# The output projection as seven block products over pairs of token tiles, with its sums and low parts spread over VectorE, ScalarE and GpSimd

## The chip, the core and the metric

The kernel runs on one NeuronCore of one Trainium2 chip. TensorE does the matrix products, VectorE (DVE in the profile), ScalarE (ACT) and GpSimd (POOL) do elementwise work, SyncE (SP) issues the DMAs. The metric is the time of one execution on the device, in microseconds (us). The kernel before takes 676.48 us in the median of three runs (676.13 to 676.74).

## The reference

One encoder layer on 1024 tokens of 1024 channels, in float32. After a LayerNorm `h`, one input projection gives the inputs of two branches, 2-D neighbourhood attention and a bidirectional RG-LRU. The part that the change touches is the end:

```python
y_a = attn * jax.nn.silu(z_a)
y_b = h * jax.nn.silu(z_b)
m = jax.nn.sigmoid(g_a + b_merge[0]) * (y_a @ w_ba) + jax.nn.sigmoid(g_b + b_merge[1]) * (y_b @ w_bb)
out = m @ w_out
return layer_norm(ALPHA * x + out, ln_g, ln_b)
```

`m` and `w_out` are 1024 x 1024, and the sum over channels is the last large product of the kernel.

## The kernel before

Every large product is made in three passes of a reduced-precision float32 format. A matrix is split into a high part (a cast, on ScalarE) and a low part (the full value minus the high part, `lo_of`, line 128). `mm3` (line 130) then issues three matmuls for each 128-channel piece: high x high, low x high and high x low, all added up in one PSUM bank of 128 x 512.

The input projection, up to about 425 us, is already done with seven block products in place of eight. Attention follows, with the products of the second branch filled in between, up to 535 us.

Then comes the **merge**, 16 slots (loop at line 1316). Slot 2j+n makes channels 128j to 128j+127 of `m` for token half n: 12 matmuls into a bank `mb`, then on VectorE the gate (`b_gate`, line 1020) and the sum with the other branch (`merge`, line 1302), on ScalarE the high part `mh`, on VectorE the low part `ml`. Between these ScalarE and GpSimd split the next slot's branch weights (`wb`) and the rows of `w_out` (`wo`, 128 x 1024 at a time, ScalarE line 1344, GpSimd line 128).

Then comes the **output projection** (loop at line 1390): for each of the 8 tiles of 128 tokens two column halves, each of 8 channel pieces x 3 = 24 matmuls (`o_product`, line 1365). The last tile's second half is done in two pieces of 256 columns. VectorE adds ALPHA times the residual (`z`, line 1399) and takes the statistics. For tiles 0 to 6, ScalarE scales (line 1408), GpSimd multiplies by the gain and adds the bias (lines 1409 and 1410) and SyncE stores the tile (line 1411). The last tile is finished on VectorE alone (lines 1416 and 1421), in four pieces that are stored one by one (line 1422).

The order of the instructions of VectorE, ScalarE, GpSimd and SyncE is that of the code (`tc.manual_schedule`): each engine works its list in order, and an instruction whose input is not there holds up all behind it. TensorE's list is in the order of the code too.

Of the kernel before, what the change touches and what calls it, by code (L numbers as in the profile page):

```python
# [10 lines left out]
F32 = mybir.dt.float32  # L11
# [56 lines left out]
def encoder_kernel(ctx, tc, x, gb1, gb, w_qk, w_v, w_s, w_ba, w_bb, w_gate, smalls, bias, w_out, out):  # L68
# [1009 lines left out]
    ya = pair(yap, [P, 4, S], "ya")  # L1078
    at0 = pool("at0")
    acc = [pst.tile([P, HALF], F32, name=f"acc{g}") for g in range(2)]  # L1080
# [104 lines left out]
    def gated(h, n):  # L1185
        hp = h // 2
        at_, (hi, lo) = attns[hp][:, halves[n]], [t[:, hp, halves[n]] for t in ya]
        G.tensor_tensor(at_, at_, gates[hp][:, halves[n]], ALU.mult)
        G.tensor_copy(hi, at_)
        lo_of(G, lo, at_, hi)  # L1190

    def last_half(g):
# [3 lines left out]
        def product(n):  # L1196
            at_ = attns[hp][:, halves[n]]
            V.tensor_tensor(at_, at_, gates[hp][:, halves[n]], ALU.mult)
            A.copy(ya[0][:, hp, halves[n]], at_)

        def low(n):
            lo_of(V, ya[1][:, hp, halves[n]], attns[hp][:, halves[n]], ya[0][:, hp, halves[n]])
# [23 lines left out]
    for unit in range(-NT, H * NT + PV_LAG):  # L1226
# [50 lines left out]
        if unit == H * NT:  # L1277
# [4 lines left out]
            wo = [pair(wop, [P, D], f"wo{k}") for k in range(NK - 2)]  # L1282
            wos = {}

            def w_load(k):
                if k < NK:
                    wos[k] = wop.tile([P, D], F32, tag="wos", bufs=3, name=f"wos{k}")
                    SP.dma_start(wos[k][:], w_out[k * P:(k + 1) * P, :])
# [4 lines left out]
            for k in range(3):  # L1293
                w_load(k)
# [3 lines left out]
    sums_m, mh, ml = {}, {}, {}  # L1298

    def merge(j, n, o):  # L1300
        b_gate(0, j, n, o)
        V.tensor_tensor(o[:], o[:], late["m", j, n][:], ALU.add)
        mh[j, n] = late["mp"].tile([P, HALF], F32R, tag=f"m{j}{n}", name=f"mh{j}{n}")
        A.copy(mh[j, n][:], o[:])

    def merge_lo(j, n, o):
        lo_of(V, ml[j, n][:], o[:], mh[j, n][:])
# [6 lines left out]
    banks[0] = pst  # L1314
    turns.append(itertools.chain(["mb", "mb", "s"], itertools.cycle(["tp", "mb", "s"])))
    for slot in range(2 * NK + 2):
        j, n = divmod(slot, 2)
        if 2 < slot <= 2 * NK:
            merge(*divmod(slot - 1, 2), sums_m[slot - 1])
        if slot == 2:  # L1320
            at0.release()
            mlp = pool("mlp")
            ml.update({(j, n): mlp.tile([P, HALF], F32R, name=f"ml{j}{n}") for j in range(NK) for n in range(2)})
            wo += [pair(mlp, [P, D], f"wo{k}") for k in range(NK - 2, NK)]
            merge_lo(0, 0, sums_m.pop(0))
        for q in (1,) if slot == 3 else (slot - 2,) if slot > 3 else ():
            merge_lo(*divmod(q, 2), sums_m.pop(q))
        if j < NK:
            if n == 0:
                b_load(0, j + 2)  # L1330
            g_load(0, j + 1, n, **(dict(tag=f"u{slot % 4}", bufs=1) if slot % 4 else dict(tag="z", bufs=5)))
            o = sums_m[slot] = bank(f"mb{j}{n}")

            run(b_group(0, j, n, ya, o, range(3 if slot < 2 else 4)))
            if 0 < slot < 3:
                run(b_group(0, 0, slot - 1, ya, sums_m[slot - 1], range(3, 4)))
            if n == 0 and j > 0:
                b_split(0, j + 1, A)
            if 0 < slot < 3:
                merge(0, slot - 1, sums_m[slot - 1])  # L1340

        if slot % 2:
            if j < NK:
                A.copy(wo[j][0][:], wos[j][:])
# [4 lines left out]
        if slot == 9:  # L1349
            zp = pool("zp")  # L1350
            gb2 = zp.tile([P, 2, D], F32, name="gb2")
            zs = {}

            def load_z(i):
                if i < NT:
                    zs[i] = zp.tile([P, D], F32, tag="z", bufs=4, name=f"z{i}")
                    SP.dma_start(zs[i][:], h_d[i])

        elif slot in (10, 12, 14):
            load_z(slot // 2 - 5)  # L1360
        elif slot in (11, 13):
            SP.dma_start(gb2[:, :, halves[slot // 13]], gb[slot // 13])
# [9 lines left out]
    def small(name, n, bufs=2):  # L1372
        return zp.tile([P, n], F32, tag=name[:2], bufs=bufs, name=name)

    def newton(mv, i, other):

        sd, ve = small(f"sd{i}", 1), small(f"ve{i}", 3)
# [12 lines left out]
    for i in range(NT):  # L1390
        last = i == NT - 1
# [117 lines left out]
```

## Time and profile before

| what | us |
| --- | --- |
| median of three runs | 676.48 |
| the profiled execution | 676.07 |
| its span, first to last instruction | 674.3 |
| merge: 192 matmuls, from 535.19 | 43.59 |
| output projection: 408 matmuls, from 578.77 | 87.36 |

In the rows that follow, a group row of the timeline gives the start, the duration, the engine, the line, the operation, out<-in, the shapes and the count; in brackets the idle time before it and what ended it. The chain of waits gives start, duration and the work that the end of the program hung on. The window rows give, for each stretch of the span, its length and then the busy time of each engine with the number of instructions.

### The profile page before, as it was taken

How to read it: one execution, taken by the hardware profiler on the slowest of the kernel's cores; microseconds unless marked ns; L12 is line 12 of the kernel's file. 1: busy time of each engine (PE TensorE's matmuls, PEld its weight loads, DVE VectorE, ACT ScalarE, POOL GpSimd, SP SyncE). 2: the span in 40 equal slices, each digit the busy share in tenths (PEclk: the TensorE clock that was granted, in tenths of full speed). 3: DMA queues.
4: the chain of work that ended last, by engine and by line, in shares of the span. 5: the costliest groups of instructions: out<-in, count | busy, mean ns of one | idle time of the engine just before them, and what ended most of it. 6: DMA issues, size and time to landing. Idle time of an engine off the chain costs nothing.

```text
span 674.3 us, 9352 instructions
## 1 busy us (share of the span) xinstructions
PE 663.7 (98%) x3189; PEld 554.3 (82%) x3189; DVE 498.9 (74%) x835; ACT 364.5 (54%) x615; POOL 354.4 (53%) x261
## 2 busy tenths in 40 slices
PE   8999999999999999999999999999999999999995
PEld 7888888888888887888788888888888888888884
DVE  6978876985998699879968785477788787443334
ACT  6555433357786676669576634477777555210110
POOL 5898263433676575567647544115255456334432
PEclk9999999999999999999999999999999999999999
DMA  8746616033344033531543557998794467412211
GB/s 322 246 152 228 209 41 221 36 125 109 126 143 150 22 108 110 172 126 48 202 172 124 172 186 261 339 332 308 251 317 146 163 232 280 170 62 94 93 63 62
DMA packets 48990, 113.40 MB, mean 168 GB/s; under 512 B 5088, under 2 KB 9776, under 8 KB 47408
## 3 DMA queue, kind: packets, MB, share of 16 engines
q1 hardware_dynamic: 48912, 112.81, 48.0%
q8 instruction: 25, 0.41, 0.2%
q14 instruction: 21, 0.17, 0.1%
q10 hardware_dynamic: 32, 0.01, 0.0%
HBM read 77.11 MB, written 35.68 MB: 167 GB/s over the span
## 4 chain that ended last, share of the span: by engine, by line
PE 76%; DVE 9%; issue 4%; POOL 1%; ACT 1%; DMA 1%; SPq 0%; DVEq 0%; POOLq 0%
PE a L134 28%; PE o L134 13%; PE mb L134 13%; PE s L134 11%; PE acc L1145 4%; PE s L1099 3%; PE pt L1121 3%; PE g L794 2%; POOL ht_l L128 1%; DVE ws_l L128 1%; DVE wa_l L128 1%; DMA a_2f<-in_w_s_dram 1%; DVE uc L752 1%; ACT ht_h L312 1%; DVE s_12f L384 0%
## 5 line engine op out<-in xcount | busy, mean ns | idle before, releaser
L134 PE MATMUL a<-ht_h,ws_h 128*128 128x512 f32 x136 | 53.1, 391 | 0.0
L134 PE MATMUL a<-ht_h,ws_l 128*128 128x512 f32 x136 | 53.0, 389 | 0.0
L134 PE MATMUL a<-b_h,wa_l 128*128 128x512 f32 x136 | 53.0, 389 | 0.0
L134 PE MATMUL a<-ht_l,ws_h 128*128 128x512 f32 x136 | 52.9, 389 | 0.0
L134 PE MATMUL a<-b_h,wa_h 128*128 128x512 f32 x136 | 52.9, 389 | 0.0
L134 PE MATMUL a<-b_l,wa_h 128*128 128x512 f32 x136 | 52.9, 389 | 0.0
L134 PE MATMUL o<-wo_h,ml 128*128 128x512 f32 (+1 forms) x136 | 51.2, 377 | 0.0
L134 PE MATMUL o<-wo_l,mh 128*128 128x512 f32 (+1 forms) x136 | 51.2, 376 | 0.0
L134 PE MATMUL o<-wo_h,mh 128*128 128x512 f32 (+1 forms) x136 | 51.2, 376 | 0.0
L1109 DVE CUSTOM_DVE_ANT_0 sc<-s,bias 128x384 f32<-128x384 f32 (+1 forms) x64 | 33.3, 522 | 21.5 <-PE s L1099 14.1
L1399 DVE SCALAR_TENSOR_TENSOR z<-z,o 128x512 f32<-128x512 f32 (+1 forms) x17 | 11.2, 656 | 51.1 <-PE o L134 51.1
L1129 ACT CAST pt_h<-pt 128x384 fp32r<-128x384 f32 x64 | 29.0, 453 | 25.3 <-PE pt L1121 17.3
L1409 POOL TENSOR_TENSOR z<-z,gb 128x1024 f32<-128x1024 f32 x7 | 16.8, 2397 | 48.6 <-ACT z L1408 48.6
L1114 ACT ACTIVATE p<-sc,summ 128x384 f32<-128x384 f32 (+1 forms) x64 | 37.8, 591 | 5.5 <-DVE summ L1109 5.3
L1378 ACT ACTIVATE sd<-mv,eps_z 128x1 f32<-128x1 f32 x8 | 2.4, 294 | 67.1 <-DVE mv L1404 67.1
L128 DVE TENSOR_TENSOR pt_l<-pt,pt_h 128x384 fp32r<-128x384 f32 x64 | 33.2, 519 | 2.1 <-ACT pt_h L1129 1.6
L326 PE MATMUL v<-wv,b_h 128*128 128x512 f32 x128 | 32.8, 398 | 0.2 <-ACT b_h L279 0.2
L902 POOL CAST wb_h<-wb 128x512 fp32r<-128x512 f32 x9 | 7.0, 778 | 49.3 <-DMA wb<-in_w_bb_dram 49.3
L128 POOL TENSOR_TENSOR ht_l<-t,ht_h 128x512 fp32r<-128x512 f32 x16 | 22.0, 1408 | 19.9 <-ACT ht_h L312 19.9
L1099 PE MATMUL s<-ks,qs 128*128 128x384 f32 (+1 forms) x128 | 31.5, 327 | 0.0
L134 PEld LDWEIGHTS a<-ht_h,ws_h 128*128 128x128 f32 x136 | 25.5, 188 | 5.9 <-issue 0.4
L1121 PEld LDWEIGHTS pt<-ident,p 128*128 128x128 f32 x176 | 23.1, 140 | 8.5
(455 smaller groups left out, 2192.4 us busy)
## 6 DMA issues: line engine op xcount, KB each, us to landing
ks<-k_d SPq DMA_DIRECT2D x8, 1024.0 KB, 8.3
h_d<-x SPq DMA_DIRECT2D x8, 512.0 KB, 5.0
v_d<-vs SPq DMA_DIRECT2D x8, 512.0 KB, 3.5
q_d<-q SPq DMA_DIRECT2D x8, 512.0 KB, 3.0
ga_d<-ga SPq DMA_DIRECT2D x16, 256.0 KB, 2.2
gb_d<-gb SPq DMA_DIRECT2D x16, 256.0 KB, 2.4
k_d<-k SPq DMA_DIRECT2D x8, 512.0 KB, 3.4
qs<-q_d SPq DMA_DIRECT2D x8, 512.0 KB, 5.2
```

Source lines behind the costliest of these rows:

```text
L128: eng.tensor_tensor(lo, full, hi.bitcast(F32), ALU.subtract)
L134: PE.matmul(o, a, b, start=first and i == 0, stop=last and i == len(prods) - 1, skip_group_check=not (first and last))
L326: PE.matmul(vos[i][:], a, wv[kind == "w"][k][:], start=vn[i] == 0, stop=vn[i] == 23)
L794: PE.matmul(o[:, n, :], w[:, 2 * d + b, :], us[b][:, n * HALF:(n + 1) * HALF], start=z == 0, stop=z == 1)
L1099: PE.matmul(o[:, :P * len(near(t))], q[:, t * P:(t + 1) * P], k[:, z, keys], start=z == 0, stop=z == 1)
L1109: V.tensor_tensor_reduce(s[:, :w], o[:, :w], heads[h][2][:, b0:b0 + w], -1.0, 3.0e38, ALU.add, ALU.min, accum_out=sums[h][0][:, t:t + 1])
L1114: A.activation(probs[h % 2][t][:], scs.pop((h, t))[:, :w], AF.Exp, bias=sums[h][0][:, t:t + 1], scale=-1.0, accum_out=sums[h][1][:, t:t + 1])
L1121: PE.transpose(tp[:, n * P:(n + 1) * P], probs[h % 2][t][:, z * P:(z + 1) * P], ident[:])
L1129: A.copy(pt[0][:, span(b)], tps[h, b][:, :P * len(near(b))])
L1145: PE.matmul(acc[g][:, d:d + w], vvs[h // 2][:, b, h % 2, :], pt[:, a:a + w], start=b in (1, 6) and z == 0, stop=z == 1 and b == (4, 7)[g])
L1399: V.scalar_tensor_tensor(z[:, cols], z[:, cols], ALPHA * TWICE, o, ALU.mult, ALU.add)
L1409: G.tensor_tensor(z[:], z[:], gb2[:, 0, :], ALU.mult)
```

## The change

The 1024 x 1024 product is cut into 2 x 2 blocks of 512. With A the merged `m` (rows are token halves 1 and 2, columns are channel halves) and B = `w_out`:

- S1 = A21 + A22, S2 = S1 - A11, S3 = A11 - A21, S4 = A12 - S2
- T1 = B12 - B11, T2 = B22 - T1, T3 = B22 - B12, T4 = B21 - T2
- C11 = A11 B11 + A12 B21; with U2 = A11 B11 + S2 T2 and U3 = U2 + S3 T3: C12 = U2 + S1 T1 + S4 B22, C21 = U3 + A22 T4, C22 = U3 + S1 T1

That is seven products where the four blocks of C need eight. Each is done for the four pairs p (token tiles p and p + 4), 28 in all, each of 4 channel pieces x 3 = 12 matmuls into one bank. Two banks for each pair (`banksX`, `banksW`) collect the sums; VectorE reads a bank out where C needs it and the next product goes on adding to it. In the program's names `b11h2` is the high part and `b11l2` the low part of channel piece 2 of B11, `z` has the pair, the token half and the column half.

Each of the seven factors on the A side and the seven on the B side needs its own high and low part. The high parts are on ScalarE. S1, S2 and S4 and their sums are made on VectorE during the merge, S3 and T1 on GpSimd, T2 on GpSimd at slot 17, T3 and T4 on VectorE. Low parts: on VectorE for A11, A22, S2, S4 and S3, the last in tiles of their own; on GpSimd for A12, B11, B21, S1, T1, T2, B22, T3 and T4. Places in SBUF are handed on: in `w_low` each low part goes where the tile lay that the low part before it was made from.

The rows of z, the gain and the bias are now loaded and handled in halves of 512 columns, so GpSimd has four operations of 128 x 512 for each of seven token tiles. `ya` becomes tiles of its own for each channel piece and token half. `jobs` is a table from slot to work; slots 0 to 15 are the merge, slots 16 to 43 the 28 products.

GpSimd, from the last slots of the merge on. Before:

```order
L128 TENSOR_TENSOR wb07_l_5937<-wb07_5868,wb07_h_5936 128x512
L128 TENSOR_TENSOR wo5_l_5563<-wos5_5807,wo5_h_5562 128x1024
L128 TENSOR_TENSOR wo6_l_5653<-wos6_5857,wo6_h_5652 128x1024
L128 TENSOR_TENSOR wo7_l_5655<-wos7_5913,wo7_h_5654 128x1024
L1409 TENSOR_TENSOR z0_5890<-z0_5890,gb2_5862 128x1024
L1410 TENSOR_TENSOR z0_5890<-z0_5890,gb2_5862 128x1024
```

Now, from the low part of the last piece of A12 (a12l3) on:

```order
L128 TENSOR_TENSOR a12l3_6060<-m170_5468,a12h3_6024 128x512
L128 TENSOR_TENSOR b21l0_6062<-wb21_0_5765,b21h0_5885 128x512
L128 TENSOR_TENSOR b21l1_6066<-wb21_1_5795,b21h1_5917 128x512
L128 TENSOR_TENSOR b21l2_6068<-wb21_2_5826,b21h2_5951 128x512
L128 TENSOR_TENSOR b21l3_6070<-wb21_3_5856,b21h3_5981 128x512
L1324 TENSOR_TENSOR t20_6096<-wb22_0_5708,t10_5683 128x512
L1324 TENSOR_TENSOR t21_6104<-wb22_1_5738,t11_5740 128x512
L1324 TENSOR_TENSOR t22_6108<-wb22_2_5769,t12_5799 128x512
L1324 TENSOR_TENSOR t23_6112<-wb22_3_5801,t13_5858 128x512
L128 TENSOR_TENSOR t2l0_6134<-t20_6096,t2h0_6098 128x512
L128 TENSOR_TENSOR t2l1_6161<-t21_6104,t2h1_6138 128x512
L128 TENSOR_TENSOR s1l0_6183<-m101_4069,s1h0_6136 128x512
```

Where one low part of `w_out` stood ahead of the first finished tile there are now 29 operations: these twelve and 17 more low parts (the rest of T2 and S1, those of T1 and B22, three of T3, one of T4). The last of T3 and three of T4 stand, two and two, behind the four operations of the first and of the second tile. The whole list from a12l3 to the last finished tile is 61 operations, all 128 x 512; T1's last low part is the 23rd of them.

VectorE, in the merge, from the bank of slot 10 to that of slot 12. Before:

```order
L1020 SCALAR_TENSOR_TENSOR mb50_5872<-g050_5816,mb50_5872 128x512
L1302 TENSOR_TENSOR mb50_5872<-mb50_5872,m150_5044 128x512
L128 TENSOR_TENSOR ml41_5645<-mb41_5843,mh41_5865 128x512
L1020 SCALAR_TENSOR_TENSOR mb51_5899<-g051_5841,mb51_5899 128x512
L1302 TENSOR_TENSOR mb51_5899<-mb51_5899,m151_5142 128x512
L128 TENSOR_TENSOR ml50_5646<-mb50_5872,mh50_5894 128x512
```

Now, the ten operations for the two slots of a channel piece in the second half of the merge:

```order
L128 TENSOR_TENSOR a22l1_5975<-mb51_5923,a22h1_5942 128x512
L1357 TENSOR_TENSOR m111_4294<-m111_4294,mb51_5923 128x512
L1324 TENSOR_TENSOR mb51_5923<-m111_4294,m110_4190 128x512
L1021 SCALAR_TENSOR_TENSOR mb61_5985<-g061_5921,mb61_5985 128x512
L1331 TENSOR_TENSOR mb61_5985<-mb61_5985,m161_5374 128x512
L128 TENSOR_TENSOR s2l1_6002<-mb51_5923,s2h1_5979 128x512
L1324 TENSOR_TENSOR mb51_5923<-m150_5058,mb51_5923 128x512
L1021 SCALAR_TENSOR_TENSOR mb70_6009<-g070_5953,mb70_6009 128x512
L1331 TENSOR_TENSOR mb70_6009<-mb70_6009,m170_5468 128x512
L128 TENSOR_TENSOR s4l1_6027<-mb51_5923,s4h1_6005 128x512
```

Two slots had six operations on VectorE and now have ten; the sums S1 (line 1357), S2 and S4 (line 1324) and three low parts stand between the gates of the banks that follow.

SyncE, the end of its list (`out` is the output, z the finished tiles). Before:

```order
L1411 DMA out_0_dram<-z3_6012 128x1024
L1357 DMA z7_6296<-h_d_89 128x1024
L1411 DMA out_0_dram<-z4_6083 128x1024
L1411 DMA out_0_dram<-z5_6154 128x1024
L1411 DMA out_0_dram<-z6_6225 128x1024
L1422 DMA out_0_dram<-z7_6296 128x256 x4
```

Now:

```order
L1497 DMA out_0_dram<-z011_6311 128x512
L1497 DMA out_0_dram<-z110_6433 128x512
L1497 DMA out_0_dram<-z111_6339 128x512
L1497 DMA out_0_dram<-z210_6473 128x512
L1497 DMA out_0_dram<-z211_6365 128x512
L1601 DMA out_0_dram<-z310_6511 128x256 x2
L1601 DMA out_0_dram<-z311_6393 128x256 x2
```

As before, the stores of the last token tile, which VectorE finishes, stand behind the stores of the tiles that GpSimd finishes.

The diff, cut to the places that the prediction speaks of:

```diff
-        yield from mm3(o[:], [([t[:, k, :] for t in b_w[which, j]], [t[:, k, halves[n]] for t in y]) for k in ks],
+        yield from mm3(o[:], [([t[:, k, :] for t in b_w[which, j]], [t[k, n][:] if which == 0 else t[:, k, halves[n]] for t in y])
+                              for k in ks],
...
-    ya = pair(yap, [P, 4, S], "ya")
+    ya = [{(k, n): yap.tile([P, HALF], F32R, tag=f"y{z}{k}{n}", name=f"ya{z}{k}{n}") for k in range(4) for n in BOTH}
+          for z in BOTH]
...
+    RING = ("mb", "mb", "s", "tp", "acc0", "s", "tp", "acc1")
...
+    def high(o, c, src, pl, tag, **kw):
+        t = hi[o, c] = place((o, "h", c), pl, tag, **kw)
+        A.copy(t[:], src)
+
+    def low(o, c, src, pl, tag, eng=V):
+        t = lo[o, c] = place((o, "l", c), pl, tag)
+        lo_of(eng, t[:], src, hi[o, c][:])
...
+    def merge(slot):
+        j, n = divmod(slot, 2)
+        c, o, m = j % 4, got[slot], late["m", j, n]
         b_gate(0, j, n, o)
-        V.tensor_tensor(o[:], o[:], late["m", j, n][:], ALU.add)
-        mh[j, n] = late["mp"].tile([P, HALF], F32R, tag=f"m{j}{n}", name=f"mh{j}{n}")
-        A.copy(mh[j, n][:], o[:])
...
-    def merge_lo(j, n, o):
-        lo_of(V, ml[j, n][:], o[:], mh[j, n][:])
...
+        dst = m if j < 4 and n else o
+        V.tensor_tensor(dst[:], o[:], m[:], ALU.add)
+
+    def split(slot):
+        j, n = divmod(slot, 2)
+        c, o, m = j % 4, got[slot], late["m", j, n]
+        if n == 0:
+            name = ("a11", "a12")[j // 4]
+            high(name, c, o[:], ap, f"{name}h{c}")
+            A.copy(m[:], o[:])
+        elif j >= 4:
+            high("a22", c, o[:], late["mp"], f"m{j}1")
...
+    def split_lo(slot):
+        j, n = divmod(slot, 2)
+        c = j % 4
+        if j < 4 and n:
+            t = raw["s3", c] = place(("s3", c), ap, f"s3l{c}", F32)
+            minus(t[:], late["m", c, 0][:], late["m", c, 1][:], G)
+            return
+        name = (("a11",), ("a12", "a22"))[j // 4][n]
+        if name == "a12":
+            low(name, c, late["m", j, 0][:], ap, f"{name}l{c}", G)
+        else:
+            low(name, c, got[slot][:], ap, f"{name}l{c}")
+
+    def second(c, o):
+        V.tensor_tensor(late["m", c, 1][:], late["m", c, 1][:], o[:], ALU.add)
+        minus(o[:], late["m", c, 1][:], late["m", c, 0][:])
+        high("s2", c, o[:], late["mp"], f"m{c}0")
+
+    def fourth(c, o):
+        low("s2", c, o[:], ap, f"s2l{c}")
+        minus(o[:], late["m", c + 4, 0][:], o[:])
+        high("s4", c, o[:], late["mp"], f"m{c + 4}0")
+
+    def fourth_lo(c, o):
+        low("s4", c, o[:], wop, f"s4l{c}")
...
-        if slot % 2:
-            if j < NK:
-                A.copy(wo[j][0][:], wos[j][:])
-            if j > 0:
-                w_load(j + 2)
-        elif slot > 0:
-            lo_of(G, wo[j - 1][1][:], wos.pop(j - 1)[:], wo[j - 1][0][:])
...
-    def o_product(i, cols):
-        o = bank(f"o{i}_{cols.start}")
-        w = cols.stop - cols.start
-        run(mm3(o[:, :w], [([t[k, i // 4][:, ti(i)] for t in (mh, ml)], [t[:, cols] for t in wo[k]])
-                           for k in range(NK)]))
-        return o[:, :w]
...
+        if slot > 1:
+            jobs.setdefault(slot + 1, [])[:0] = [lambda s=slot: merge(s), lambda s=slot: split(s)]
+        job(slot + 2, split_lo, slot)
+        if n and j >= 4:
+            job(slot + 2, lambda c, s: second(c, got[s]), j - 4, slot)
+            job(slot + 3, lambda c, s: fourth(c, got[s]), j - 4, slot)
+            job(slot + 4, lambda c, s: fourth_lo(c, got[s]), j - 4, slot)
...
+    def t1(c):
+        t = raw["t1", c] = place(("t1", c), wop, f"t1{c}", F32)
+        minus(t[:], raw["b12", c][:], raw["b11", c][:], G)
+
+    def t2(c):
+        t = raw["t2", c] = place(("t2", c), yap, f"y0{c}1", F32)
+        minus(t[:], raw["b22", c][:], raw["t1", c][:], G)
+
+    def t3(c):
+        t = raw["t3", c] = raw["b12", c]
+        minus(t[:], raw["b22", c][:], t[:])
+
+    def t4(c):
+        t = raw["t4", c] = raw["b21", c]
+        minus(t[:], t[:], raw["t2", c][:])
...
+    spare, homes = [(wop, "spare")], {}
+
+    def w_low(o, c, full, *home):
+        homes[o, c] = spare.pop()
+        spare.append(home)
+        low(o, c, full[:], *homes[o, c], G)
...
+        job(2 * c + 3, t1, c)
...
+        job(2 * c + 5, lambda c: w_low("b11", c, raw["b11", c], wop, f"b11{c}"), c)
...
+        job(16, lambda c: low("b21", c, raw["b21", c][:], yap, f"y1{c}1", G), c)
...
+        job(17, t2, c)
+        job(18 + c, t4, c)
...
+        job(18 + c, lambda c: w_low("t2", c, raw["t2", c], yap, f"y0{c}1"), c)
...
+        job(20 + c, lambda c: w_low("s1", c, late["m", c, 1], late["mp"], f"m{c}1"), c)
+        job(24 + c, t3, c)
...
+        job(22 + c, lambda c: w_low("t1", c, raw["t1", c], wop, f"t1{c}"), c)
+        job(24 + c, lambda c: w_low("b22", c, raw["b22", c], wop, f"b22{c}"), c)
...
+        job(28 + c, lambda c: w_low("t3", c, raw["t3", c], wop, f"b12{c}"), c)
...
+        job(27 + c, lambda c: low("s3", c, raw["s3", c][:], *((ap, f"s3l{c - 1}") if c else (wop, "spare3"))), c)
...
+        job(30 + c, lambda c: w_low("t4", c, raw["t4", c], wop, f"b21{c}"), c)
...
+            z = zs[p, r, n]
             A.activation(z[:], z[:], AF.Identity, bias=ve[:, 2:3], scale=sd[:])
-            G.tensor_tensor(z[:], z[:], gb2[:, 0, :], ALU.mult)
-            G.tensor_tensor(z[:], z[:], gb2[:, 1, :], ALU.add)
-            SP.dma_start(out[i], z[:])
+            G.tensor_tensor(z[:], z[:], gbs[0, n][:], ALU.mult)
+            G.tensor_tensor(z[:], z[:], gbs[1, n][:], ALU.add)
+            SP.dma_start(out[p + 4 * r][:, halves[n]], z[:])
...
+    LAST = [("s3", "t3", 0), ("s3", "t3", 1), ("a22", "t4", 0), ("s3", "t3", 2), ("a22", "t4", 1), ("s3", "t3", 3),
+            ("a22", "t4", 2), ("a22", "t4", 3)]
+    PLAN = [("a11", "b11", range(4)), ("a12", "b21", range(4)), ("s2", "t2", range(4)), ("s1", "t1", (0, 1)),
+            ("s4", "b22", (0, 1)), ("s1", "t1", (2, 3)), ("s4", "b22", (2, 3))]
...
+        a, b, p = plan[slot - 16]
+        if a == "a11":
+            banksX[p] = ring(slot, f"x{p}")
+        elif a == "a12":
+            banksW[p] = ring(slot, f"w{p}")
+        if slot < 16 + len(plan) - 1:
+            o = banksX[p] if a in ("a11", "s2", "s3", "a22") else banksW[p]
+            o_product(a, b, p, o[:], first=a in ("a11", "a12", "s1"), last=a in ("a12", "s4", "a22"))
...
+        o_product("a22", "t4", p, o[:, :256], part)
+        V.tensor_tensor(w[:, part], zs[p, 1, 0][:, part], o[:, :256], ALU.add)
```

More of the change, by code (lines that the diff above doesn't have):

```diff
@@ L1281, in encoder_kernel, with w_load @@
             wop = pool("wop", "right")
[L1282 to L1288, printed above, removed]
+            raw = {}
+            def w_load(o, c):
+                k, n = ("b11", "b12", "b21", "b22").index(o) // 2 * 4 + c, int(o[2]) - 1
+                t = raw[o, c] = wop.tile([P, HALF], F32, tag=f"{o}{c}", name=f"w{o}_{c}")
+                SP.dma_start(t[:], w_out[k * P:(k + 1) * P, halves[n]])
             b_load(0, 1)
@@ L1313, in encoder_kernel @@
     assert not todo
-    banks[0] = pst
-    turns.append(itertools.chain(["mb", "mb", "s"], itertools.cycle(["tp", "mb", "s"])))
-    for slot in range(2 * NK + 2):
+    for slot in range(16):
         j, n = divmod(slot, 2)
[L1318 to L1327, printed above, removed]
-        if j < NK:
[L1329 to L1340, printed above, removed]
-        if slot % 2:
-            if j < NK:
-                A.copy(wo[j][0][:], wos[j][:])
-            if j > 0:
-                w_load(j + 2)
-        elif slot > 0:
-            lo_of(G, wo[j - 1][1][:], wos.pop(j - 1)[:], wo[j - 1][0][:])
[L1349 to L1362, printed above, removed]
@@ L1423, in encoder_kernel @@
+    sd, ve = newton(mv, "last", scaled())
+    for n, part in pieces:
+        z = zs[p, 1, n]
+        V.scalar_tensor_tensor(z[:, part], (w, x)[n][:, part], sd[:], gbs[1, n][:, part], ALU.mult, ALU.add)
+        SP.dma_start(out[p + 4][:, halves[n]][:, part], z[:, part])
     order.__exit__(None, None, None)
-    for pl in (zp, mlp, yap, late["mp"], cst, wop, late["wb"], ev, dram, banks[0]):
+    for pl in (zp, ap, yap, late["mp"], cst, wop, late["wb"], ev, dram, pst):
         pl.release()
```

178 lines of the change are left out of this document (140 added, 38 removed).

## The prediction

> **What bounds the kernel now.** I read the page's first lines, then the end of the chain of waits, then busy time by stretches of the span.
>
> ```profile
> span 674.3 us, 9352 instructions
> PE 663.7 (98%) x3189; PEld 554.3 (82%) x3189; DVE 498.9 (74%) x835; ACT 364.5 (54%) x615; POOL 354.4 (53%) x261
> ...
> 535.19 43.59 PE mb L134 x192
> 578.77 87.36 PE o L134 x408
> 670.26 0.79 DVE z L1421 x2
> ```
>
> TensorE sets the end: from 535.19 the chain lies on it without a gap until the last product. 192 matmuls in 43.59 us are 0.2270 each and 2.724 for a slot of 12. The 408 of the output projection are 360 of 512 columns and 48 of 256, worth 384 full ones: 87.36 / 384 = 0.2275 each.
>
> ```profile
> 535.00:579.00 44.00, 44.00 (x196) 36.35 (x195) 34.21 (x51) 21.77 (x34) 27.98 (x16) 1.00 0.78 279
> 579.00:666.00 87.00, 87.00 (x408) 72.95 (x406) 32.70 (x79) 12.73 (x17) 35.95 (x15) 1.00 0.19 72
> 666.00:674.30 8.30, 0.12 (x2) 0.00 (x0) 4.79 (x15) 0.29 (x1) 0.00 (x0) 0.80 0.25 84
> ```
>
> After the engines' columns stand the granted clock (1.00), the DMA share and GB/s. In the merge VectorE is busy 34.2 of 44 us; in the output projection VectorE, ScalarE and GpSimd are busy 33, 13 and 36 of 87. That is the room the change works in. The last 8.3 us are VectorE finishing the last tile and its stores.
>
> **The products taken out.** 28 products of 12 matmuls are 336 where 384 were: 48 x 0.2275 = 10.9 us less on TensorE. If it stayed the bound, 676.5 would become 665.6. What must be shown is whether the others keep up.
>
> **ScalarE** gets 28 more casts behind 578.8 (about 0.6 each, below): 17 us into 74 us of room, hidden. **VectorE** behind 578.8 gets some 35 more operations of about 0.69 (T3, T4, S3's low parts, what is left over from the merge, 28 banks read out where there were 17): 24 us into 54, hidden too, except that GpSimd meets them. **SyncE** moves the same bytes in halves of 256 KB, issued slots ahead: no time. If a load came late, it would cost its lateness.
>
> **VectorE in the merge.** How quickly its operations follow each other:
>
> ```profile
> 565.21 0.70 DVE L1020 SCALAR_TENSOR_TENSOR mb<-g,mb 128x512 f32<-128x512 f32 x1 [0.70 <-PE mb L134]
> 565.94 0.70 DVE L1302 TENSOR_TENSOR mb<-mb,m 128x512 f32<-128x512 f32 x1
> 566.55 0.68 DVE L128 TENSOR_TENSOR ml<-mb,mh 128x512 fp32r<-128x512 f32 x1
> ...
> 566.68 0.59 ACT L1304 CAST mh<-mb 128x512 fp32r<-128x512 f32 x1 [1.61 <-DVE mb L1302]
> 567.16 1.05 ACT L1344 CAST wo_h<-wos 128x1024 fp32r<-128x1024 f32 x1
> ```
>
> An operation that needs the one before it starts 0.73 after it, another 0.61 after it. ScalarE's next cast starts 0.48 after the last. Two slots take TensorE 5.45 us; the ten operations that VectorE now has for them in the second half of the merge take 3 x 0.73 + 7 x 0.61 = 6.5. So VectorE falls behind from slot 11 on. Slot 10's bank is taken at 565.2, as in the first row. From there to the sum of slot 14 are 21 operations: 7 x 0.73 + 13 x 0.61 + 0.70 for the last, and about 0.7 of waiting for GpSimd (below), 14.4 in all: 579.6. ScalarE then casts A12's last piece and copies it (0.48 + 0.59): 580.7. GpSimd can take a12l3 at **580.8**. TensorE is not held: it multiplies A11 and A12 meanwhile.
>
> **GpSimd**, the term that decides.
>
> ```profile
> 21.52 5.28 POOL L259 TENSOR_TENSOR x<-x,gb 128x512 f32<-128x512 f32 x4 [1.24 <-ACT x L253]
> ...
> 544.72 1.29 POOL L128 TENSOR_TENSOR wb_l<-wb,wb_h 128x512 fp32r<-128x512 f32 x1 [6.03 <-ACT wb_h L900]
> 545.97 2.41 POOL L128 TENSOR_TENSOR wo_l<-wos,wo_h 128x1024 fp32r<-128x1024 f32 x1
> ```
>
> An operation of 128 x 512 is followed by the next after 545.97 - 544.72 = 1.25. The first row is the same pair that ends each tile, gain then bias, on two halves: 5.28, where four free ones would take 3 x 1.25 + 1.29 = 5.04. So an operation that needs the one just before it costs 0.12 more.
>
> Then there is VectorE's claim on GpSimd:
>
> ```profile
> 52.65 4.26 POOL L128 TENSOR_TENSOR ht_l<-t,ht_h 128x512 fp32r<-128x512 f32 x3
> 53.25 1.25 DVE L301 TENSOR_TENSOR t<-t,b_l 128x512 f32<-128x512 f32 x1
> ...
> 535.92 1.61 DVE L1198 TENSOR_TENSOR attn<-attn,za 128x512 f32<-128x512 f32 x1
> 536.93 1.76 POOL L128 TENSOR_TENSOR wb_l<-wb,wb_h 128x512 fp32r<-128x512 f32 x1
> ...
> 539.16 0.68 DVE L1198 TENSOR_TENSOR attn<-attn,za 128x512 f32<-128x512 f32 x1
> ```
>
> With both inputs in SBUF, VectorE's operation took 1.61 beside GpSimd and 0.68 alone: it waited for GpSimd's operation to end. GpSimd's next one then took 1.76 in place of 1.29; in the first pair three took 4.26 in place of 3.79. A meeting costs GpSimd 0.47; counted from start to start I take **0.45**. Bounds: nothing, and VectorE's whole 0.69.
>
> The list from a12l3 has 61 operations: 33 low parts and sums, then gain and bias for seven tiles in four pieces, 28. Each follows at 1.25: 60 x 1.25 + 1.29 = 76.3. The 14 bias operations need the one before, and so do 21 low parts, since each goes where the source of the last one lay. VectorE meets the list 14 times with two SBUF inputs: two sums of S2, four of T4, four of T3, four low parts of S3. Eleven of these fall ahead of a low part that waits anyway. That leaves 24 x 0.12 + 14 x 0.45 = 9.2.
>
> One wait is left, for the first tile:
>
> ```profile
> 589.69 0.69 DVE L1399 SCALAR_TENSOR_TENSOR z<-z,o 128x512 f32<-128x512 f32 x1 [4.02 <-PE o L134]
> ...
> 592.72 1.25 ACT L1408 ACTIVATE z<-z,ve,sd 128x1024 f32<-128x1024 f32 x1 [1.04 <-DVE ve L1407]
> ```
>
> From the sum with the residual to the scaling is 3.03; scaling a half I put at 0.7 (an estimate from 1.25 for 1024). T1's last low part is the list's 23rd: 580.8 + 22 x 1.25 + 4 x 0.12 + 12 x 0.45 + 1.3 = 615.5. TensorE wants it in the last matmul of slot 28, which would start at 578.77 + 13 x 2.724 - 0.23 = 613.95, and so **stands 1.6**. Slot 30 then ends at 615.5 + 0.2 + 5.45 = 621.2, and the first half is scaled by 621.2 + 0.1 + 3.03 + 0.7 = 625.0. GpSimd has been free since 580.8 + 29 x 1.25 + 8 x 0.12 + 14 x 0.45 = 624.3, and waits 0.7 to 0.9. It ends at 580.8 + 76.3 + 9.2 + 0.9 = **667.2**. TensorE is done by 578.77 + 28 x 2.724 + 1.6 = 656.6, and is no longer the bound.
>
> There is a floor under this. Without any meeting TensorE does not stand, slot 30 ends at 619.6 and the first half is scaled at 623.4; the 32 operations from there on take 32 x 1.25 + 16 x 0.12 = 41.9 and end at 665.3. Start and meetings can gain 1.9 us at most.
>
> **The end.**
>
> ```profile
> 661.90 2.41 POOL L1410 TENSOR_TENSOR z<-z,gb 128x1024 f32<-128x1024 f32 x1
> ...
> 664.34 0.33 SPq L1411 DMA_DIRECT2D out_dram<-z  x1
> ...
> 669.89 1.79 SPq L1422 DMA_DIRECT2D out_dram<-z  x4
> ```
>
> SyncE issues a store 0.03 after GpSimd ends. VectorE has finished the last tile by about 662.4 (TensorE's end and, as now, some 5 us), but its four stores stand behind GpSimd's last one. So the end is 667.2 + 0.03 + 0.4 for one issue + the 4.4 us from the first of the four (669.89) to the span's end (674.3): **672.05**, 2.25 less than 674.3. The profiled execution took 676.07, the median is 676.48; on the median that is 674.2.
>
> So of 10.9 us some 8.7 are given back, because GpSimd, with 36 of 87 us filled now, gets 86 us of work that may not start before 580.8.
>
> **Rivals.** *Whole-instruction blocking.* If VectorE's operation keeps GpSimd out for all its 0.69, the 14 meetings cost 14 x 0.24 = 3.4 more: 677.6, no change. Against it stand the two rows above, 0.47 each; for it, that only these meetings were looked at and that GpSimd is now never idle. The Trainium skill, SBUF — State Buffer, "Who interferes with whom", says this: the engine that comes first has the shared pair for the whole instruction and the other fully blocks. This trace shows that VectorE waits in full, and GpSimd for about two thirds of VectorE's operation.
>
> *TensorE stays the bound*, 665.6 to 667. It asks that GpSimd be done by about 660.6, 4.7 us under the floor. Only operations at 1.1 us would do that, and no row shows one.
>
> *Slower: GpSimd starves TensorE already in the merge.* In slots 3 to 12 its list has for every two slots a low part of the branch weights, a sum of T1, one of S3 and a low part of B11: 4 x 1.25 = 5.0 of 5.45 us. At 1.37 each it is 5.5, just even. If they take 1.70, as one does that meets VectorE (1.25 + 0.45), it is 6.8: over four rounds 5.4 us too much.
>
> ```profile
> 559.70 1.29 POOL L128 TENSOR_TENSOR wb_l<-wb,wb_h 128x512 fp32r<-128x512 f32 x1 [1.79 <-ACT wb_h L900]
> ```
>
> Now this low part is there at 561.0, 1.4 before slot 10 begins (535.19 + 10 x 2.724 = 562.4). Less that, TensorE and all behind it come 4.0 later, at 678.2. Against it: VectorE has no operation with two SBUF inputs between 541 and 568. For it: T1 waits for loads of `w_out`, with a DMA share of 0.78 there. It makes the kernel slower from about 1.68 an operation.
>
> *The change doesn't do what it says*: the matmuls are 336 in the program's order, so this has no chance of its own.
>
> **How the numbers follow.** GpSimd as the bound at the measured prices, 0.68: 674.2, own range 672.3 (the floor) to 676.2 (half the dearer meetings, or 2 us of late start). Whole blocking 0.15, starving in the merge 0.13, TensorE as the bound 0.04. A measurement of this kernel can tell about 0.2%, 1.35 us, from no change: faster is under 675.1, slower over 677.8. Of the forecast 0.55 lies under 675.1, 0.12 within and 0.01 over; of whole blocking 0.12 within and 0.03 over; of the slower case 0.02 and 0.11; the fourth is faster. Faster 0.59, no change 0.26, slower 0.15. The range for 8 in 10, 671.9 to 677.7, reaches from just under the floor to whole blocking.
>
> **What would show it.** Right: GpSimd almost without a gap from about 581 to 667, with gain and bias pairs 2.62 apart; idle times of TensorE near 614 and nowhere else over half a microsecond; the chain of waits ending on GpSimd's z and SyncE rather than on TensorE; VectorE idle at the end before the stores go. Wrong in the start: a12l3 far from 580.8, so VectorE's lag is mis-sized. Wrong in the price: operations on GpSimd at 1.9 where VectorE meets them, or idle TensorE between 541 and 579. If TensorE ends at 655 and the span 8 us later, GpSimd was not the bound, and the forecast is wrong in kind.

## The result and the profile after

| | median, us | lowest to highest | runs |
| --- | --- | --- | --- |
| before | 676.48 | 675.18 to 677.04 | 9 |
| changed | 674.3 | 673.15 to 675.27 | 9 |

The ratio is 0.9969, 95% interval [0.9958, 0.9979]: faster by 0.3%, of the 1.6% that 48 matmuls fewer could have brought. The profiled execution took 674.84, its span is 673.0. In this execution the merge already began 0.7 later than in the one shown of before (535.89 for 535.19; in the ten experiments' profiles, which share the changed code up to there, it begins between 534.17 and 535.52). The difference is chance, so 0.7 is added to the prediction's start times where they are compared with it below.

First the page's opening and then, in the chain of waits, what the end hung on from the merge on (a few of its rows):

```profile
span 673.0 us, 9451 instructions
PE 652.1 (97%) x3129; PEld 543.1 (81%) x3129; DVE 529.2 (79%) x872; ACT 384.6 (57%) x662; POOL 403.6 (60%) x315
```

```profile
535.89 43.57 PE mb L134 x192
579.46 10.88 PE x L134 x48
590.34 10.88 PE w L134 x48
601.22 8.20 PE x L134 x36
610.05 1.76 DVE s3l L128
611.81 1.71 DVE wb L1324
614.74 1.59 POOL t1l L128
...
664.23 1.26 POOL z L1496
```

TensorE still looks like the bound by its share, 97%, one point less than before. The chain says otherwise: it lies on TensorE up to about 609, then on two operations of VectorE that meet GpSimd and take 1.76 and 1.71 in place of 0.68 (a low part of S3, a sum of T3), and from 614.74 on GpSimd to the last gain and bias, but for its wait for the first tile at 625. By stretches (length, then busy time of TensorE, weight loads, VectorE, ScalarE, GpSimd):

```profile
579.00:666.00 87.00, 77.09 (x351) 63.72 (x349) 67.41 (x132) 33.54 (x59) 81.03 (x60) 0.97 0.26 88
666.00:673.00 7.00, 0.00 (x0) 0.00 (x0) 0.00 (x0) 0.00 (x0) 1.97 (x2) 0.50 0.43 150
```

TensorE went from 87.00 to 77.09 of these 87 us, GpSimd from 35.95 to 81.03. Of the 9.9 us that TensorE is idle, 1.8 are one stand (a wait in the middle of its products) and 8.1 lie behind its last matmul. The list of waits for the same time has, of the waits that the prediction counted, these (waited for; total, times, longest):

```profile
POOL a12l L128 <- ACT m L1339: 5.6, 1, 5.6
...
PE w L134 <- POOL t1l L128: 1.8, 1, 1.8
POOL z L1495 <- ACT z L1494: 1.1, 1, 1.1
```

And the timeline at GpSimd's start, at a meeting with VectorE, at the first finished tile and at the end:

```profile
581.18 1.29 POOL L128 TENSOR_TENSOR a12l<-m,a12h 128x512 fp32r<-128x512 f32 x1 [5.60 <-ACT m L1339]
...
609.97 1.30 POOL L128 TENSOR_TENSOR b22l<-wb,b22h 128x512 fp32r<-128x512 f32 x1
610.05 1.76 DVE L128 TENSOR_TENSOR s3l<-s,s3h 128x512 fp32r<-128x512 f32 x1
611.34 1.62 POOL L128 TENSOR_TENSOR t1l<-t,t1h 128x512 fp32r<-128x512 f32 x1
613.04 1.62 POOL L128 TENSOR_TENSOR b22l<-wb,b22h 128x512 fp32r<-128x512 f32 x1
...
626.32 1.30 POOL L1495 TENSOR_TENSOR z<-z,gb 128x512 f32<-128x512 f32 x1 [1.13 <-ACT z L1494]
...
663.36 0.87 DVE L1600 SCALAR_TENSOR_TENSOR z<-x,sdlast,gb 128x256 f32<-128x256 f32 x2
...
666.79 1.26 POOL L1496 TENSOR_TENSOR z<-z,gb 128x512 f32<-128x512 f32 x1
668.50 1.86 SPq L1601 DMA_DIRECT2D out_dram<-z  x4
```

VectorE's low part of S3 starts at 610.05 and takes 1.76 instead of 0.68, since it waits for GpSimd's operation that began at 609.97. GpSimd's next one takes 1.62 instead of 1.29, and the one behind it starts 1.70 after it, where 1.37 is the pitch without a meeting. At the end VectorE is done at 664.2, GpSimd at 668.05, and only then come VectorE's four stores. GpSimd's list from a12l3 to its end is 668.05 - 581.18 = **86.87** us long. This length is free of the shift of 0.7, and the experiments are compared by it too.

### The profile page after: what moved, and what is told of

Same layout as the page of the kernel before. It is cut to its first block, busy times and chain, and to the rows that moved or that the text cites. A ratio compares the mean times of both kernels' runs of the same rounds, so it can differ in the third digit from the quotient of the medians.

```text
span 673.0 us, 9451 instructions
## 1 busy us (share of the span) xinstructions
PE 652.1 (97%) x3129; PEld 543.1 (81%) x3129; DVE 529.2 (79%) x872; ACT 384.6 (57%) x662; POOL 403.6 (60%) x315
## 4 chain that ended last, share of the span: by engine, by line
PE 67%; DVE 9%; POOL 9%; issue 4%; ACT 1%; DMA 1%; SPq 0%; POOLq 0%; DVEq 0%; ACTq 0%
PE a L134 28%; PE mb L134 13%; PE s L134 11%; PE acc L1147 4%; PE s L1101 3%; PE x L134 3%; PE pt L1123 3%; POOL z L1495 3%; POOL z L1496 2%; PE g L794 2%; PE w L134 2%; POOL ht_l L128 1%; DVE ws_l L128 1%; DVE wa_l L128 1%; POOL t3l L128 1%
## 5 line engine op out<-in xcount | busy, mean ns | idle before, releaser
L1116 ACT ACTIVATE p<-sc,summ 128x384 f32<-128x384 f32 (+1 forms) x64 | 37.8, 591 | 5.3 <-DVE summ L1111 5.0
L134 PE MATMUL mb<-ya,wb_h 128*128 128x512 f32 x128 | 39.6, 389 | 0.0
L134 PEld LDWEIGHTS a<-b_h,wa_h 128*128 128x128 f32 x136 | 25.5, 188 | 5.4
L134 PEld LDWEIGHTS a<-ht_l,ws_h 128*128 128x128 f32 x136 | 25.5, 188 | 5.4
L134 PEld LDWEIGHTS a<-b_l,wa_h 128*128 128x128 f32 x136 | 25.5, 188 | 5.3
L134 PEld LDWEIGHTS a<-b_h,wa_l 128*128 128x128 f32 x136 | 25.5, 188 | 5.3
L134 PEld LDWEIGHTS a<-ht_h,ws_l 128*128 128x128 f32 x136 | 25.5, 188 | 5.2
```

The costliest lines, as they stand in the source:

```text
L134: PE.matmul(o, a, b, start=first and i == 0, stop=last and i == len(prods) - 1, skip_group_check=not (first and last))
L1116: A.activation(probs[h % 2][t][:], scs.pop((h, t))[:, :w], AF.Exp, bias=sums[h][0][:, t:t + 1], scale=-1.0, accum_out=sums[h][1][:, t:t + 1])
```

## The experiments

All ratios are to the kernel before, run on the same chip (its medians there: 675.5 for e1 to e4, 676.22 for e5 to e8, 675.48 for e9 and e10). The last column but one is the difference of the ratio from the change's 0.9969, in us of 676; each ratio is uncertain by 0.001 to 0.0015, so such a difference is uncertain by some 1.1 us (an estimate), and what is said of the small ones rests on the length of GpSimd's list. The list has 61 operations in the change, 47 in e1, 53 in e3, 57 in e8 and 59 in e9.

| | median | ratio, 95% interval | against the change | GpSimd's list |
| --- | --- | --- | --- | --- |
| change | 674.3 | 0.9969 [0.9958, 0.9979] | | 86.87 |
| e1 no bias | 668.5 | 0.9896 [0.9881, 0.9911] | -4.9 | 80.69 |
| e2 no sums | 671.58 | 0.9940 [0.9927, 0.9954] | -2.0 | 84.78 |
| e3 T2, B21 on VectorE | 676.69 | 1.0016 [1.0007, 1.0025] | +3.2 | 89.63 |
| e4 gain and bias apart | 671.81 | 0.9945 [0.9932, 0.9957] | -1.6 | 85.23 |
| e5 seven meetings | 676.5 | 1.0005 [0.9996, 1.0014] | +2.4 | 89.18 |
| e6 seven, one input | 674.84 | 0.9980 [0.9971, 0.9989] | +0.7 | 87.62 |
| e7 stores on ScalarE's queue | 671.95 | 0.9939 [0.9927, 0.9952] | -2.0 | 88.49 |
| e8 lighter GpSimd | 667.82 | 0.9874 [0.9860, 0.9887] | -6.4 | 80.83 |
| e9 two S1 lows on VectorE | 671.59 | 0.9939 [0.9925, 0.9952] | -2.0 | 84.83 |
| e10 seven statistics | 673.58 | 0.9970 [0.9958, 0.9982] | +0.1 | 86.90 |

**e1: is GpSimd the bound?** In the seven tiles that GpSimd finishes:

```diff
             G.tensor_tensor(z[:], z[:], gbs[0, n][:], ALU.mult)
-            G.tensor_tensor(z[:], z[:], gbs[1, n][:], ALU.add)
```

> Leaves out the bias addition of the seven row tiles that GpSimd finishes (14 of its operations; the last tile keeps its bias). Theory (GpSimd sets the end): 14 x 1.25 to 1.31 = 17.5 to 18.3 us go from the queue that ended at 668.05; GpSimd then follows ScalarE's scaling and ends near 661, the end falls to VectorE, which ended at 664.2, and its four stores, which took 3.7 us behind VectorE's last operation in the kernel before: span about 668, median about 669. Rival (TensorE, 97% busy, still sets the end): nothing changes, 674 to 674.5.

The median fell by 4.9, the span to 666.9. GpSimd now waits for ScalarE before its last tiles instead of working through a queue; the timeline has, for the last of them and for SyncE's last stores:

```profile
658.69 2.49 POOL L1495 TENSOR_TENSOR z<-z,gb 128x512 f32<-128x512 f32 x2 [3.16 <-ACT z L1494]
...
662.43 1.79 SPq L1600 DMA_DIRECT2D out_dram<-z  x4
```

With GpSimd out of the way the end is VectorE's (663.58). TensorE, as busy as before, does not set it in the changed kernel. The rival falls.

**e2: what do the meetings cost?** `t3` and `t4` keep their input and leave out the subtraction (`t4` is shown, `t3` likewise):

```diff
-        t = raw["t4", c] = raw["b21", c]
-        minus(t[:], t[:], raw["t2", c][:])
+        raw["t4", c] = raw["b21", c]
```

> Leaves out the eight sums T3 and T4 on VectorE (each reads two SBUF tiles); the block products then use the parts of B12 and B21 as they stand. GpSimd's own operations stay as many. Theory (a meeting costs GpSimd about 0.45, and what is saved ahead of the first finished tile only shortens TensorE's stand): T4's four meetings fall away ahead of the first finished tile and take TensorE's 1.6 us of standing with them, so the first finished tile comes 1.6 earlier and GpSimd ends 1.5 to 2 earlier: span 671.2, median 672.5. Rival 1 (each of the eight meetings lies on the chain that sets the end, at 0.45): 3.6 less, median 670.7. Rival 2 (GpSimd is held for the whole of each VectorE operation, 0.69): 5.5 less, median 668.8.

2.0 less. TensorE no longer stands, and GpSimd's wait for the first finished tile grows from 1.1 to 2.1:

```profile
POOL z L1493 <- ACT z L1492: 2.1, 1, 2.1
```

GpSimd's work from a12l3 up to that tile takes 40.9 us in place of 44.0. Of these 3.1, which are 0.39 for each of the eight meetings, 1.0 turned into waiting for the tile and 2.1 came out. That GpSimd now waits 2.1 there although six meetings are left is the floor of the prediction ("start and meetings can gain 1.9 us at most"). Both rivals, which add up all eight meetings, fall.

**e3: one part undone.** T2's sums and B21's low parts back on VectorE:

```diff
-        minus(t[:], raw["b22", c][:], raw["t1", c][:], G)
+        minus(t[:], raw["b22", c][:], raw["t1", c][:])
```
```diff
-        job(16, lambda c: low("b21", c, raw["b21", c][:], yap, f"y1{c}1", G), c)
+        job(16, lambda c: low("b21", c, raw["b21", c][:], yap, f"y1{c}1"), c)
```

> Undoes one part: T2's four sums and the four low parts of B21 go back to VectorE, all else stays. Theory (VectorE is the late engine at the end of the merge, about 15 us behind its work): the eight operations, 0.69 each and up to 1.2 where they meet GpSimd, come late, T2's parts with them; TensorE stands 3 to 5 us between 597 and 620, and although GpSimd has eight operations fewer it ends later, since its 28 last ones begin with the first finished tile: span 674 to 677, median 675 to 678. Rival (the number of GpSimd's operations sets the end): 8 x 1.3 = 10.4 us off its queue, the end falls to VectorE at 664 to 666, median 669 to 671.

Eight operations fewer on GpSimd, and 3.2 us slower. GpSimd's list of waits shows where they went:

```profile
POOL t2l L128 <- ACT t2h L1317: 10.1, 1, 10.1
POOL t2l L128 <- DVE s4l L128: 4.2, 1, 4.2
```

VectorE's timeline has the eight operations that came back to it:

```profile
583.74 2.49 DVE L128 TENSOR_TENSOR b21l<-wb,b21h 128x512 fp32r<-128x512 f32 x4
...
589.27 3.58 DVE L1324 TENSOR_TENSOR t<-wb,t 128x512 f32<-128x512 f32 x4
```

They stand among what is left over from the merge, T2's sums only at 589.27. GpSimd sits idle for 14.3 us meanwhile, and TensorE stands 0.6 and 1.75 us for T2's low parts, less than the 3 to 5 of the theory. T1's last low part ends 37.8 us behind the start of a12l3 where it was 35.2, the first finished tile comes as much later, and the 32 operations from there on take 41.8 us as before (41.7). The rival, which only counts operations, falls. What counts is not how many operations GpSimd has, but how many are left when the first tile is finished.

**e4: the dependence.** All gains of a tile ahead of its bias additions:

```diff
             G.tensor_tensor(z[:], z[:], gbs[0, n][:], ALU.mult)
+        for n in range(2):
+            z = zs[p, r, n]
             G.tensor_tensor(z[:], z[:], gbs[1, n][:], ALU.add)
```

> Same operations; for each of GpSimd's seven tiles the two gains come first and then the two bias additions, so that no bias addition reads what the operation just before it wrote. Theory (a GpSimd operation that reads the one before it starts 0.12 later): 14 x 0.12 = 1.7 us less on GpSimd, its pitch in the last 40 us goes from 1.31 to 1.25, it ends near 666.4, span 671.3, median 672.6. Rival (1.31 is the pitch whatever it reads): no change, 674.3.

1.6 less, the list 1.64 shorter; the rival falls. GpSimd's last rows, two operations each:

```profile
660.43 2.52 POOL L1495 TENSOR_TENSOR z<-z,gb 128x512 f32<-128x512 f32 x2
662.87 2.51 POOL L1498 TENSOR_TENSOR z<-z,gb 128x512 f32<-128x512 f32 x2
```

Two operations now last 2.52, start of the first to end of the second; in the change's last pair they last 2.60 (665.45 to 668.05). The order of two lines is worth as much as 1.3 operations.

**e5, e6, e10: the price of a meeting, and which operations meet.** Behind each tile's store, one more operation on VectorE, whose result nobody reads:

```diff
             SP.dma_start(out[p + 4 * r][:, halves[n]], z[:])
+        for n in range(1):
+            junk = place(("junk", p, r, n), late["mp"], "m00", F32)
+            V.tensor_tensor(junk[:], gbs[0, n % 2][:], gbs[1, n % 2][:], ALU.add)
```

That is e5. In e6 the last line is `V.tensor_scalar(junk[:], gbs[0, n % 2][:], 2.0, 1.0, ALU.mult, ALU.add)`, in e10 `V.bn_stats(junk[:], gbs[0, 0][:])` with six columns of result.

> Adds to VectorE, behind each of the seven tiles that GpSimd finishes, one addition of two SBUF tiles (128x512, 0.69 us alone) whose result nobody reads; GpSimd's operations stay the same. Theory (a meeting holds GpSimd for 0.45 of the 0.69, and less where the 0.12 gap ahead of a bias addition lies under it): 6 or 7 meetings x 0.33 to 0.45 = 2.0 to 3.2 us on GpSimd's end, 670 to 671.2 instead of 668.05, span 675 to 676.2, median 676.3 to 677.4. Rival 1 (GpSimd is held for the whole of VectorE's operation): 6 or 7 x 0.57 to 0.69 = 3.4 to 4.8, median 677.7 to 679.1. Rival 2 (the two engines do not hold each other, the 1.6 seen elsewhere has another cause): no change, 674.3.

> The same seven places, but the added VectorE operation reads one SBUF tile (tensor x 2 + 1, 128x512). Theory (only operations of VectorE with two inputs in SBUF meet GpSimd): GpSimd's operations keep their pitch of 2.62 a pair, its end stays at 668.05 and the median at 674.3. Rival (any VectorE operation on SBUF holds GpSimd): as with two inputs, 676.3 or more.

> A third kind of VectorE operation in the same seven places: statistics of one SBUF tile (128x512, 0.70 us, the operation that VectorE runs all through this stage). Theory (only those VectorE operations hold GpSimd that read a second stream from SBUF: two inputs, or the one-input arithmetic that ran at 0.42 for 512 columns): pairs keep 2.62, median 674.3 and no statistics operation longer than 0.70. Rival (any VectorE operation on SBUF holds GpSimd and is held): GpSimd loses 0.2 to 0.45 at each place, 1.3 to 3 us in all, and the statistics last 1.1 us or more where GpSimd is busy.

The added operations, in nanoseconds (shortest/median/longest), of e5, e6 and e10 in this order:

```profile
L1500 DVE TENSOR_TENSOR junk<-gb,gb x7: 680/1439/1734, 624.9 to 660.7; 128x512 f32<-128x512 f32 x7
```
```profile
L1500 DVE TENSOR_SCALAR junk<-gb x7: 419/1093/1493, 624.4 to 658.8; 128x512 f32<-128x512 f32 x7
```
```profile
L1499 DVE BATCH_NORM_STATS2 junk<-gb x7: 685/686/687, 624.0 to 657.1; 128x6 f32<-128x512 f32 x7
```

And what one meeting does to GpSimd, in the timeline of e5 and then of e6:

```profile
648.11 1.30 POOL L1495 TENSOR_TENSOR z<-z,gb 128x512 f32<-128x512 f32 x1
648.48 1.48 DVE L1500 TENSOR_TENSOR junk<-gb,gb 128x512 f32<-128x512 f32 x1
...
649.48 1.63 POOL L1496 TENSOR_TENSOR z<-z,gb 128x512 f32<-128x512 f32 x1
```
```profile
646.79 1.30 POOL L1495 TENSOR_TENSOR z<-z,gb 128x512 f32<-128x512 f32 x1
647.15 1.22 DVE L1500 TENSOR_SCALAR junk<-gb 128x512 f32<-128x512 f32 x1
...
648.17 1.36 POOL L1496 TENSOR_TENSOR z<-z,gb 128x512 f32<-128x512 f32 x1
```

In e5 six GpSimd operations are longer, five of them 1.63 to 1.75 alone, and the list grows by 89.18 - 86.87 = 2.31: 0.39 each, inside the theory's 2.0 to 3.2 and below the 3.4 of the rival that puts all of VectorE's operation on GpSimd. TensorE also stands 1.4 once for VectorE in e5, but GpSimd has no wait behind the first tile, so this isn't in the list. In e6 the theory fails: the one-input operation meets GpSimd too. It lasts 0.42 alone and 1.09 in the median, so it waits for GpSimd as the two-input one does, and GpSimd's longer operations take 1.36 to 1.48 for 1.29; the list grows by 0.75. Its rival (676.3 or more) fails as well, with 674.84 and a third of the price of two inputs in the list. e10's statistics, one input as well and longer (0.69), never wait, and the list stays at 86.90, as its theory said. So it is not the number of tiles read from memory. The Trainium skill, SBUF — State Buffer, "Who interferes with whom", says that `tensor_scalar` can enter modes of VectorE that take the port pair which it shares with GpSimd; e6 agrees, by its 1.09 us for 0.42. The same section lets the loser block for the whole of the other's instruction. VectorE does. GpSimd lost only 0.34 to 0.46 of 0.68, and 0.07 to 0.19 of 0.42, but its ends fit a full block too. In the rows above VectorE's operation ends 0.55 (e5) and 0.28 (e6) behind the GpSimd operation that it waited for (649.96 for 649.41, 648.37 for 648.09), and GpSimd's next one ends 1.15 and 1.16 behind VectorE's end. All five single meetings of each run give the same, 0.54 to 0.56 or 0.28 to 0.29, and then 1.12 to 1.17. So GpSimd's operation ends at a fixed time behind VectorE's, whatever the kind, and what it loses goes with how much of VectorE's operation is left when its own turn comes. The price is measured; that GpSimd works on beside VectorE is not shown.

**e7: the issue behind the last store.**

```diff
-        SP.dma_start(out[p + 4][:, halves[n]][:, part], z[:, part])
+        A.dma_start(out[p + 4][:, halves[n]][:, part], z[:, part])
```

> Issues the last tile's four stores on ScalarE's queue instead of SyncE's, nothing else. Theory (the four stores stand behind GpSimd's last store on SyncE though VectorE was done 4 us earlier, and what they cost is their issue behind it): the end is then GpSimd's last store alone, 668.05 + 0.4 + about 2.6 = 671.1 instead of 673.0: median 672.4 to 672.7. Rival (the stores' way through memory sets the end, not their issue): no change, 674.3.

2.0 less, a little over the 1.6 to 1.9 of the theory and within the interval; the rival falls. In the profiled execution the span ends 3.15 behind GpSimd (668.35 to 671.5) where it was 4.95. That GpSimd's list is longer there has another cause, at the end of this document.

**e9 and e8: the stand, and all together.**

```diff
-        low(o, c, full[:], *homes[o, c], G)
+        low(o, c, full[:], *homes[o, c], V if (o, c) in (("s1", 1), ("s1", 2)) else G)
```

> Of the four edits of the lighter version the first alone: two of S1's four low parts on VectorE instead of GpSimd. Theory (TensorE's stand at 614 is GpSimd's lateness, and the first finished tile and with it GpSimd's last 28 operations hang on that stand): the stand of 1.8 goes, GpSimd's first gain starts 1.6 to 1.9 earlier, its end moves as much: 666.2 to 666.5, span 671.2, median 672.4 to 672.7. Rival (VectorE, which waits out GpSimd at its two-input operations, brings the two low parts later than GpSimd did): TensorE stands as long as before or longer, median 674.3 or more.

2.0 less, a little more than the 1.6 to 1.9 of the theory and within the interval; no wait of TensorE for GpSimd is left in the list, and the rival falls. VectorE did wait for it, 2.6 and 1.2 us for the places of the two low parts, at times when it had that to spare.

e8 adds e4's and e7's edits, and for the second half of the tile (2, 1), which GpSimd finished last:

```diff
+    (mv, sd), z = late["end"], zs[2, 1, 1]
+    V.scalar_tensor_tensor(z[:], z[:], mv[:, 0:1], gbs[0, 1][:], ALU.subtract, ALU.mult)
+    V.scalar_tensor_tensor(z[:], z[:], sd[:], gbs[1, 1][:], ALU.mult, ALU.add)
+    SP.dma_start(out[2 + 4][:, halves[1]], z[:])
```

> Four edits together, nothing left out: two of S1's four low parts on VectorE instead of GpSimd (2 x 1.37 off the chain ahead of the first finished tile, and TensorE's stand of 1.6 us with them); gains and bias additions of a tile apart (1.6); the second half of the last tile that GpSimd finishes done by VectorE behind its own last tile (2 x 1.25 off GpSimd, 2 x 0.69 more on VectorE); the last tile's stores on ScalarE's queue (1.6). Theory (GpSimd's queue from the merge's end on, and the issue behind it, is all that holds the end above TensorE's): GpSimd ends near 662.5, VectorE near 664, span 667 to 668, median 668.2 to 669. Rival (work given to VectorE comes back as waiting, since its operations with two SBUF inputs wait out GpSimd's): VectorE ends at 666 to 667, median 670 to 671.5.

667.82, ratio 0.9874 [0.9860, 0.9887]: 8.4 us faster than before, and computing all of it. Its chain of waits:

```profile
535.13 43.63 PE mb L134 x192
578.75 10.88 PE x L134 x48
589.63 10.88 PE w L134 x48
600.51 10.88 PE x L134 x48
611.39 21.78 PE w L134 x96
633.17 19.05 PE x L134 x84
```

TensorE is the bound again, without a gap from the merge to 652.2; what follows is VectorE finishing the last tiles, to 662.9, while GpSimd is done at 661.3. The theory holds, and the gain against the change, 6.4, is a little over the 5.3 to 6.1 of its range; the rival falls. On GpSimd's list the edits add up: 1.64 (e4) + 2.04 (e9) + 2 x 1.25 for the half tile are 6.2, and it is 86.87 - 80.83 = 6.04 shorter. In the median they don't quite: the three edits that ran alone gave 2.0 + 1.6 + 2.0 = 5.6, and with the half tile it is 6.4, since the end has passed from GpSimd to VectorE. Of TensorE's 10.9 us 8.4 now reach the end; the rest lies behind its last matmul, from where it takes 11.0 us to the end of the span in place of 8.2.

## Why the prediction was right, step by step

- **GpSimd as the bound**: shown by the chain and by e1. e8 shows the other half of it: with GpSimd lighter, TensorE's gain comes out.
- **Its start.** a12l3 at 581.18; predicted 580.8, with the shift 581.5. VectorE falls behind in the merge at 0.73 and 0.61 as reckoned. Slot 14's sum, which A12's last piece waits for, is the row of 579.29 here:

```profile
565.90 0.70 DVE L1021 SCALAR_TENSOR_TENSOR mb<-g,mb 128x512 f32<-128x512 f32 x1 [1.29 <-PE mb L134]
...
579.29 0.70 DVE L1331 TENSOR_TENSOR mb<-mb,m 128x512 f32<-128x512 f32 x1
```

- **Its prices.** 61 operations in 86.87 us, predicted 86.4. The 0.12 of a dependent operation was confirmed by e4 (1.64 for 14). A meeting was 0.33 ahead of an operation that waits anyway (1.70 for 1.37, the 0.45 less the 0.12 as reckoned), and in the whole of e2 0.39. The remaining 0.5 is the wait for the first tile (1.1 for 0.9) and some 0.2 in the operations.
- **TensorE's stand**: predicted 1.6, was 1.8, and nowhere else. e9 moved it away, and the first finished tile and the end came earlier with it, as the step said.
- **The floor**: e2 gained 2.0 where 1.9 was the most; the stand that fell away was 1.8 and not 1.6.
- **The end.** 4.95 from GpSimd's end to the span's, predicted 4.83. That the four stores stand behind GpSimd's last one is shown by e7. VectorE was done at 664.2, predicted 663.1 with the shift, and the prediction's own terms, 656.6 + 5, give 661.6 where it wrote 662.4. VectorE doesn't wait for GpSimd there: it works from 652.85 with one wait of 0.51 for ScalarE, and comes to the last product's halves at 658.27 and 659.26, so it ends 6.4 behind TensorE in place of 5. Nothing hung on it.
- **The rivals.** Whole-instruction blocking at its price of 0.69 falls by e5. The prediction read from the rows that GpSimd is held for two thirds of VectorE's operation; that is what it loses, and the ends in e5 and e6 leave open that it is held to VectorE's end. TensorE as the bound falls by e1. Starving in the merge did not occur: the list of waits has no other wait of TensorE behind 579, and the chain lies on it through the merge.
- **What the prediction had wrong**: it counted a meeting by two inputs in SBUF. e6 shows that a one-input operation can meet as well. This cost nothing here, since behind the merge VectorE has no such operation of that width.
- **The sum.** 672.05 for the span against 673.0, which is 0.25 over when the shift is taken off, and 674.2 against a median of 674.3. The terms are off by -0.3 (the start), +0.5 (the list) and +0.1 (the end), and partly cancel. That the medians agree to 0.1 is luck: the runs of the changed kernel spread over 2.1 us.

## What to carry to other kernels

A product saved on the busiest engine is worth only as much as the engine that prepares and finishes for it has room, and that room counts from when its work can start: here an engine that was 41% busy in a stage got 86 us of work for 87 us, and most of the gain went there. So write out that engine's list with its first possible start, and its end, before saving matmuls; and then look for what lies behind its last operation, since a queue that is shared by two producers lets the one that is ready wait for the other. Moving work to another engine pays where that engine is not late itself (e9), and costs where it is (e3), whatever the count of operations says.

## What the hardware showed that was not expected

**Behind a short stand TensorE's clock was halved twice.** In e7's profiled execution the stand of 1.76 us was followed by this (the granted clock is the third number from the end):

```profile
612.00:616.00 4.00, 2.24 (x10) 1.55 (x9) 2.28 (x4) 2.94 (x4) 3.84 (x3) 1.00 0.01 2
616.00:620.00 4.00, 4.00 (x13) 3.09 (x12) 0.97 (x3) 0.00 (x0) 3.77 (x4) 0.57 0.01 4
620.00:624.00 4.00, 4.00 (x19) 3.31 (x18) 2.59 (x4) 0.00 (x0) 3.69 (x3) 1.00 0.00 0
```

Eight matmuls came at 0.43 instead of 0.23, so the first tile was finished 1.6 later and GpSimd's list was 1.6 longer. This execution took 673.31, the four others of the kernel 671.37 to 672.17. e3's profile has the same behind its stand of 1.75, at 0.50 for 606 to 608; there another stand of 0.56 ends three matmuls ahead of it. In six other profiles (the change, e1, e4, e5, e6 and e10) a stand of the same length left the clock at 1.00. The Trainium skill, TensorE: Matmul & The Clock Gate, "HAM oscillation — how this bites in real kernels", warns of gaps over about 3.4 us; here half of that was enough in two executions of eight. What decides it no run here shows, and that the stand is the cause is inferred from the order in time.

**GpSimd gets a little quicker when TensorE ends.** Its 128x512 operation takes 1.29 to 1.30 up to there and 1.26 to 1.27 behind it. In the changed kernel the last matmul ends at 657.9:

```profile
656.49 1.30 POOL L1496 TENSOR_TENSOR z<-z,gb 128x512 f32<-128x512 f32 x1
657.75 1.27 POOL L1495 TENSOR_TENSOR z<-z,gb 128x512 f32<-128x512 f32 x1
```

In e5 it ends at 659.2, and the row of 658.00 takes 1.30, that of 659.25 takes 1.26. The cause is open.
